# A hybrid attention/SSD layer: another order of the seven products, h kept in DRAM, and attention's result added by transfers

## The chip, the cores and the metric

The kernel runs on one core of a Trainium2 chip. The metric is the device time of one execution in microseconds (us); of several runs the median is given. Five engines work side by side, each through its own list of instructions in order: PE (TensorE: matrix products from SBUF into the PSUM banks), DVE (VectorE), ACT (ScalarE), POOL (GpSimd) and SP (SyncE, which here only issues transfers). An engine that has come to an instruction whose input isn't there waits with it, and all that stands behind it on that engine waits too. Transfers between DRAM and SBUF are issued on SP's queue (`dma` in the code) or on POOL's (`store`).

## The reference

One layer of a streaming encoder for two groups of requests, 1024 tokens of a prompt and 8 x 16 tokens of samples, 1152 in all, at a width of 1024:

```python
h = rms_norm(x, norm_g) * (1 + scale) + shift            # scale, shift, gate from silu(c) @ w_ada + b_ada
q, k, v, z_att, z_ssd, xbc, dt_raw, gates = split(h @ w_in)
att_branch = (attention(q, k, v) * silu(z_att)) @ w_att_proj           # 1024 -> 1024
y = ssd_scan(silu(conv(xbc)), dt, a) + d_skip * xs                     # 16 pairs of heads, 4 groups
ssd_branch = (rms_norm(y * silu(z_ssd)) * ssd_norm_g) @ w_ssd_proj     # 2048 -> 1024
g_att, g_ssd = split(gates)
merged = sigmoid(g_att) * att_branch + sigmoid(g_ssd) * ssd_branch
out = x + gate * (merged @ w_out)
```

Keys, values, convolution rows and the SSD state are outputs too.

## The kernel before

All is kept with channels on the 128 partitions and the 1152 tokens along a row, so that a tile of eight is 128 x 1152 in fp32 (576 KB). For precision a matrix product is made of three in fp16: both operands are split into a high and a low half (hi and lo; ScalarE rounds, L694 for weights and L2173 for operands; VectorE takes the remainder, L695 and L2175), and TensorE does hi x hi, hi x lo and lo x hi (L854, L855, L856).

**Stages.** First come h and its norm, then eight attention units (until about 650 us), then sixteen pairs of SSD heads (until about 1270), whose results go to DRAM (`att_d`, `y_d`). The last stage consists of dense products alone: eight plain blocks of gates (`gate_dense`), then **quads**. A quad, `quad_dense` (L834), computes two blocks of 128 output channels for all tokens from 1024 channels with seven products instead of eight: the operand pair is cut in four quarters (`quarters`), `differences` (L2182) forms their sums on VectorE, and the seven combinations of them are multiplied with seven combinations of weights (`quad_sums` prepares these early, in the SSD stage, and keeps them in DRAM as `sum_d`). One product has 4 steps of k, 2 banks of 288 columns and 3 matmuls each: 24 matmuls. There are twenty quads, five groups of four: the other gates, attention's projection (`att_dense`), the SSD projection in two halves of the operands (`ssd_dense(0)`, `ssd_dense(1)`), and the output projection (`out_dense`).

**Banks.** A quad uses three pairs of PSUM banks: `fore` (tag `d` or the double bank `s`, alternating from quad to quad), `side` (tag `g`) and `lone` (the one of `d` and `s` that `fore` is not). Products 0, 5, 6, 3 add up in `fore`, 4 and 2 in `side`, and 1 stands alone. Between them a bank is read out while its sum goes on: `kept` (L864) copies it to SBUF on ScalarE (L873) or adds it to a base on VectorE (L869, only in `ssd_dense(1)`), `joined` (L876) adds it to what was kept (L879). The next product on a bank can't start before it was read. The order was 0, 4, 5, 1, 6, 2, 3. The first quad of a group (`wide`) does products 0, 4 and 1 step by step of k side by side, since its operands come into being one after the other; it then runs 2 ahead of 6 and gives 3 a bank of its own.

**Operands.** `pieces` (L2194) turns a pair of tiles into the seven operands of one step of k: four sums of squares on ScalarE (L686, for a check of the range), three splits of 1152 columns and one of 576, and four additions on VectorE (L2184 to L2187). For the gates `h_pieces` (L2214) first puts h together, hi + lo, with one VectorE addition per tile (L2220, eight in all). For attention `att_prep` loads `att_d`; for the SSD `ssd_prep` loads `y_d` and scales it by the norm (L2261). The operands of the output stage come from `ssd_dense(1)`: in `second` the SSD result, held in tile a (which was loaded from `acc_d`, what the first half left), is multiplied by its gate (L2329), added to attention's result in tile m (L2330; m is loaded from `att_o`), and m goes to `pieces`. So the last step of k of the output stage waits for the last output of the last SSD quad.

**Weights.** SP loads raw weights into three places (`w_ahead`), four parts of 512 KB for a quad (two from `in_quad`, two from `sum_d`). `quad_split` splits a part into hi and lo; all seven buffers of a quad are taken at once, and given back at its end (`w_done`); `w_next` splits parts of the next quad at four points of a quad.

**Order.** The program is written by generators that run against a rough clock (`pause`), and then put in order: the class `Order` (L140) has a cost for each instruction and simulates the five engines. Whenever an engine is free, it takes of the instructions that are ready by the simulation, and ready by a safe margin if there are such, the one that stands earliest in the program (`at`); instructions in `fill` count as 600 places later. The resulting order of every engine is fixed. So the order follows planned times; on the chip an engine keeps it, even when a transfer comes later than planned. If a check of the values' range fails at the end, a general kernel would run; it doesn't here.

## Time and profile before

| | us |
|---|---|
| median of 3 runs (1721.12 to 1727.28) | 1721.31 |
| profiled execution | 1722.93 |
| its span, first to last instruction | 1721.0 |
| PE busy | 1677.3 |
| DVE busy | 1378.6 |
| ACT busy | 1061.5 |
| POOL busy | 391.5 |

The profile is of one execution. Busy times count a matmul from its start to its modelled end, and these overlap. A row of a group shows the line, the engine, the operation, the tiles (output <- input; `arena` is the whole of SBUF, `d`, `g` and `s` the PSUM banks), the shape, the count, the busy time and the mean of one, and after the bar the engine's idle time just before them and what ended it. A row of the timeline has the start, the length and in brackets the idle time before it.

### The profile page before, as it was taken

Reading aid. Unit: us, or ns where it says so; the run is one execution under the profiler, and the core shown is the slowest. Engines: PE = TensorE matmul, PEld = TensorE weight load, DVE = VectorE, ACT = ScalarE, POOL = GpSimd, SP = SyncE. Lnnn points to the kernel's source line nnn. Section 1 sums busy time; section 2 is a strip of 40 time slices with the busy share of each in tenths; the row PEclk is TensorE's granted clock in tenths of the full one; section 3 lists DMA queues with packets and bytes.
Section 4 is the critical chain, followed back from the end, with each engine's and each line's share of the span. In section 5 each row is a group of like instructions: output and inputs, shape, how many; then the busy total and the mean of one; then the engine's idle time right before and its main releaser. Section 6 shows DMA issues by size and latency. Waiting matters only on the chain.

```text
span 1721.0 us, 36673 instructions
## 1 busy us (share of the span) xinstructions
PE 1677.3 (97%) x14265; PEld 1122.4 (65%) x14265; DVE 1378.6 (80%) x2546; ACT 1061.5 (62%) x2130; POOL 391.5 (23%) x640
## 2 busy tenths in 40 slices
PE   7999999999999999999999999999999999999998
PEld 3556565556565556666666666666667677777776
DVE  6458767878777888989988989996898487878963
ACT  8766556566565567456655756666388575775550
POOL 0134233135133101322321333242231011110000
PEclk9999999999999999999999999999999999999999
DMA  9248789797988688686858767878658786777651
GB/s 383 83 120 212 169 227 228 169 230 189 210 227 189 168 190 228 184 220 199 196 182 271 231 184 242 238 217 272 226 166 294 266 292 207 254 284 259 221 194 58
DMA packets 299105, 369.16 MB, mean 214 GB/s; under 512 B 211676, under 2 KB 213096, under 8 KB 298920
## 3 DMA queue, kind: packets, MB, share of 16 engines
q1 hardware_dynamic: 281896, 307.65, 63.7%
q0 software_dynamic: 17024, 59.06, 9.4%
q8 instruction: 114, 1.87, 0.5%
q14 instruction: 71, 0.58, 0.1%
HBM read 244.08 MB, written 74.06 MB: 185 GB/s over the span
## 4 chain that ended last, share of the span: by engine, by line
PE 51%; DVE 18%; DMA 11%; ACT 11%; issue 7%; POOL 1%; SPq 1%; DVEq 0%; ACTq 0%; POOLq 0%
PE d L945 6%; PE d L948 6%; PE d L946 6%; PE d L998 5%; PE d L1000 5%; PE d L999 5%; ACT arena L686 3%; PE g L1604 2%; DVE arena L2175 2%; DMA arena<-in_quad_dram 2%; DMA arena<-acs_d 2%; DVE arena L695 2%; DVE arena L1802 2%; ACT arena L1988 1%; DMA arena<-sum_d 1%
## 5 line engine op out<-in xcount | busy, mean ns | idle before, releaser
L945 PE MATMUL d<-arena 128*128 128x384 f16 x1320 | 431.0, 327 | 1.4 <-ACT arena L1779 1.4
L948 PE MATMUL d<-arena 128*128 128x384 f16 x1320 | 430.3, 326 | 0.6 <-DVE arena L695 0.6
L946 PE MATMUL d<-arena 128*128 128x384 f16 x1320 | 430.3, 326 | 0.0
L686 ACT ACTIVATE arena<-arena 128x1024 bf16<-128x1024 f32 (+4 forms) x217 | 199.3, 918 | 141.9 <-DMA arena<-in_wall_dram 96.4
L695 DVE SCALAR_TENSOR_TENSOR arena<-arena 128x1024 f16<-128x1024 f32 (+2 forms) x157 | 181.7, 1165 | 42.4 <-ACT arena L694 42.2
L694 ACT ACTIVATE arena<-arena 128x1024 f16<-128x1024 f32 (+2 forms) x157 | 155.1, 994 | 66.5 <-DMA arena<-sum_d 33.1
L945 PEld LDWEIGHTS <-arena 128*128 128x128 f16 x1320 | 129.2, 98 | 90.2 <-issue 13.3
L998 PE MATMUL d<-arena 128*128 128x384 f16 (+1 forms) x568 | 186.8, 329 | 0.0
L1000 PE MATMUL d<-arena 128*128 128x384 f16 (+1 forms) x568 | 186.1, 328 | 0.0
L999 PE MATMUL d<-arena 128*128 128x384 f16 (+1 forms) x568 | 186.1, 328 | 0.0
L948 PEld LDWEIGHTS <-arena 128*128 128x128 f16 x1320 | 129.1, 98 | 86.3 <-DVE arena L695 1.0
L946 PEld LDWEIGHTS <-arena 128*128 128x128 f16 x1320 | 129.2, 98 | 78.5 <-issue 1.6
L1544 ACT ACTIVATE arena<-arena 128x640 f32<-128x640 f32 (+4 forms) x144 | 100.8, 701 | 63.5 <-DVE arena L1547 63.1
L855 PEld LDWEIGHTS <-arena 128*128 128x128 f16 x1120 | 109.7, 98 | 43.9 <-issue 16.3
L854 PE MATMUL d<-arena 128*128 128x288 f16 x440 | 126.3, 287 | 3.7 <-ACT arena L873 3.2
L856 PEld LDWEIGHTS <-arena 128*128 128x128 f16 x1120 | 109.8, 98 | 30.5 <-issue 2.7
L854 PEld LDWEIGHTS <-arena 128*128 128x128 f16 x1120 | 110.0, 98 | 29.5 <-issue 1.7
L855 PE MATMUL d<-arena 128*128 128x288 f16 x440 | 126.2, 287 | 1.1 <-DVE arena L2175 1.1
L856 PE MATMUL d<-arena 128*128 128x288 f16 x440 | 126.1, 287 | 0.0
L854 PE MATMUL s<-arena 128*128 128x288 f16 x360 | 102.9, 286 | 6.5 <-ACT arena L873 3.9
L1802 DVE SCALAR_TENSOR_TENSOR arena<-arena 128x1176 f32<-128x1176 f32 x72 | 103.2, 1434 | 5.5 <-ACT arena L1799 3.8
L2175 DVE SCALAR_TENSOR_TENSOR arena<-arena 128x1152 f16<-128x1152 f32 (+1 forms) x72 | 87.4, 1219 | 21.9 <-ACT arena L2173 21.7
(278 smaller groups left out, 3565.0 us busy)
## 6 DMA issues: line engine op xcount, KB each, us to landing
arena<-in_quad_dram SPq DMA_DIRECT2D x80, 512.0 KB, 5.7
arena<-in_wall_dram SPq DMA_DIRECT2D x77, 512.0 KB, 5.2
sum_d<-arena POOLq DMA_DIRECT2D x40, 512.0 KB, 4.7
arena<-sum_d SPq DMA_DIRECT2D x40, 512.0 KB, 4.8
arena<-acs_d SPq DMA_DIRECT2D x32, 576.0 KB, 5.8
arena<-in_kc_dram SPq DMA_DIRECT2D x64, 256.0 KB, 4.6
arena<-in_vc_dram SPq DMA_DIRECT2D x64, 256.0 KB, 2.9
arena<-in_wada_dram SPq DMA_DIRECT2D x24, 512.0 KB, 10.2
```

The source lines that it names most:

```text
L686: keep(nc.scalar.activation(junk[:, :n], x, AF.Square, scale=scale * n ** -0.5, accum_out=sums[:, c:c + 1]))
L694: keep(nc.scalar.activation(hi, x, AF.Copy, scale=scale))
L695: keep(nc.vector.scalar_tensor_tensor(lo, x, scale, hi, ALU.mult, ALU.subtract))
L854: nc.tensor.matmul(ps, wh, xh[:, c], start=first and k == 0, stop=False, skip_group_check=not first)
L855: nc.tensor.matmul(ps, wh, xl[:, c], start=False, stop=False, skip_group_check=not first)
L856: nc.tensor.matmul(ps, wl, xh[:, c], start=False, stop=k == 3, skip_group_check=not first)
L945: nc.tensor.matmul(ps, hi.r[:, wc], kh.r[:, tok], start=k == 0, stop=False)
L946: nc.tensor.matmul(ps, hi.r[:, wc], kl.r[:, tok], start=False, stop=False)
L948: nc.tensor.matmul(ps, lo.r[:, wc], kh.r[:, tok], start=False, stop=k == nk - 1)
L998: nc.tensor.matmul(ps, kh.r[:, tok], wh, start=k == 0, stop=False)
L999: nc.tensor.matmul(ps, kh.r[:, tok], wl, start=False, stop=False)
L1000: nc.tensor.matmul(ps, kl.r[:, tok], wh, start=False, stop=k == KT - 1)
```

## The change

- **Order of products** in a quad: 0, 4, (product 3 of the quad before), 5, 1, 2, 6, and product 3 is put off (`pending`, `flush`) to the next quad, where it runs behind 0 and 4 (in an interleaved first quad behind the first step of k). Ahead of the output stage, behind its last quad, and where the next operands aren't there yet, it runs at once. `lone` is now one bank `d` and one bank `g`. In an interleaved first quad the order of the rest is as in the others, with no bank of its own for product 3.
- **Priority**: instructions that read out banks (`quick`) count as 300 places earlier in the order, with a margin of 200 ns behind them.
- **Weights**: a quad's buffers are taken part by part and given back as soon as their last product is written (`w_used`); `w_next` may split for the quad after the next.
- **h**: `h_whole` makes the eight additions in pairs 1 to 4 of the SSD stage (as `fill`), stores the tiles to `h_d` on POOL's queue, and `h_pieces` loads them on SP's. The two places of `L_SUM` grow to 1152 columns for that, and the `pad` of 576 in `L_SSD` goes, by which the SSD's tiles no longer lie on the places of the last stage's.
- **Attention's result**: for three of the four quads of `ssd_dense(1)`, attention's result is no longer loaded into a tile and added on VectorE; a transfer on POOL's queue reads `att_o` and adds it to tile a (`accum_op`), and a goes to `pieces`, 9000 ns of the rough clock later. For the fourth quad the two tiles are loaded (`att_last`) and added as before.
- **Times**: the modulation's gate (`mod_gate`, eight loads of 512 KB) begins with the gates instead of with attention's projection; the pause ahead of the SSD norm's token sums is 12000 instead of 4500; loads ahead are released tile by tile.

```diff
@@ Order
+    FAST = 300
+    SAFE_FAST = 200.0
-            u["at"] = u["i"] + self.FILL * (u["ins"][0].name in self.fill)
+            u["fast"] = u["ins"][0].name in self.fast
+            u["at"] = u["i"] + self.FILL * (u["ins"][0].name in self.fill) - self.FAST * u["fast"]
-                    m = self.SAFE_DMA if v["dma"] else self.SAFE[u["eng"]]
+                    m = self.SAFE_DMA if v["dma"] else self.SAFE_FAST if u["fast"] else self.SAFE[u["eng"]]
@@ h
+    def h_whole(k):
+
+        b = yield from walloc(L_SUM, "s", NT)
+        fill.add(nc.vector.tensor_tensor(b.ap, hhi[k].ap, hlo[k].ap, ALU.add).ins.name)
+        yield from pause(1500)
+        store(h_d[k], b.ap)
+        stored(b)
...
-                nc.vector.tensor_tensor(t.ap, hhi[k].ap, hlo[k].ap, ALU.add)
+                dma(t.ap, h_d[k])
@@ quad_dense
+        if not ops:
+            yield from flush()
+        fore, side = bank(2 if odd else 0), bank(1)
...
         yield from product(0, fore)
         p1 = yield from kept(fore, 0, 0)
         yield from product(4, side)
         p5 = yield from kept(side, 1, 1)
+        yield from flush()
+        w_next(i)
         yield from product(5, fore, first=False)
+        w_used(i, 3, 4)
         u2 = yield from kept(fore, 0, 1)
         w_next(i)
-        if not wide:
-            lone = bank(0 if odd else 2)
+        lone = lone or bank(3)
         yield from product(1, lone)
+        w_used(i, 0, 1)
         yield from joined(0, 0, p1, lone)
         w_next(i)
-        if wide:
-            yield from product(2, side, first=False)
+        yield from product(2, side, first=False)
+        yield from joined(0, 1, u2, side)
         yield from product(6, fore, first=False)
+        w_used(i, 5, 6)
+        yield from joined(1, 1, p5, fore)
         w_next(i)
...
+        def rest():
             yield from product(3, fore, first=False)
+            w_used(i, 2)
             yield from evict(1, 0, [(g * HC, HC, ps) for g, ps in enumerate(fore)], None) or ()
-        w_done(i)
+        pending.append(rest)
@@ ssd_dense, second
-                m = yield from taken("att", c + o)
+                m = a if c < 6 else (yield from taken("att", o))
...
-                nc.vector.tensor_tensor(m.ap[:, tok], m.ap[:, tok], a.ap[:, tok], ALU.add)
+                if c < 6:
+                    nc.gpsimd.dma_start(a.ap[:, tok], att_o[c + o][:, tok], accum_op=ALU.add)
+                else:
+                    nc.vector.tensor_tensor(m.ap[:, tok], m.ap[:, tok], a.ap[:, tok], ALU.add)
...
-                        urgent.append(pieces(tiles["att"][c], m, out_ops, 0.5 * SM / (SA * SW)))
+                        def last(c=c, m=m):
+                            if c < 6:
+                                yield from pause(9000)
+                            yield from pieces(tiles["acc"][c] if c < 6 else tiles["att"][0], m, out_ops, 0.5 * SM / (SA * SW))
+                        urgent.append(last())
@@ the list of stages
+        if 1 <= p < 5:
+            items[-1][1].extend(h_whole(k) for k in range(2 * p - 2, 2 * p))
-    items.append((gates_dense(), [h_pieces(), att_prep()], [], 0.5))
-    items.append((att_dense(), [tile_loads(4, ("ga", gate_d, 0)), ssd_prep(), mod_gate()], [], 0.5))
+    items.append((gates_dense(), [mod_gate(), h_pieces(), att_prep()], [], 0.5))
+    items.append((att_dense(), [tile_loads(4, ("ga", gate_d, 0)), ssd_prep()], [], 0.5))
     items.append((ssd_dense(0), [], [], 0.5))
-    items.append((ssd_dense(1), [tile_loads(3, ("acc", acc_d, 0), ("gs", gate_d, 8), ("att", att_o, 0))], [], 0.5))
+    items.append((ssd_dense(1), [tile_loads(3, ("acc", acc_d, 0), ("gs", gate_d, 8)), att_last()], [], 0.5))
```

142 lines of the change are left out of this document (79 added, 63 removed).

## The prediction

> **What bounds the kernel now.** I read the page first, then busy time by stage, then what TensorE waited for, and only then single stalls with the engine that was late.
>
> ```profile
> span 1721.0 us, 36673 instructions
> PE 1677.3 (97%) x14265; PEld 1122.4 (65%) x14265; DVE 1378.6 (80%) x2546; ACT 1061.5 (62%) x2130; POOL 391.5 (23%) x640
> PEclk9999999999999999999999999999999999999999
> ...
> GB/s 383 83 120 212 169 227 228 169 230 189 210 227 189 168 190 228 184 220 199 196 182 271 231 184 242 238 217 272 226 166 294 266 292 207 254 284 259 221 194 58
> ```
>
> TensorE is busy for 1677.3 of 1721.0 us at nearly full clock. The change neither adds nor removes a matmul, so it can only win part of the missing 43.7 us. The stages, by the windows view (length, then busy us and count of PE, PEld, DVE, ACT, POOL; PEclk, DMA share, GB/s):
>
> ```profile
> 650.00:900.00 250.00, 249.40 (x1947) 165.65 (x1940) 226.07 (x335) 158.78 (x285) 67.80 (x101) 1.00 0.71 200
> 950.00:1000.00 50.00, 50.00 (x428) 33.52 (x427) 49.44 (x82) 37.70 (x71) 19.78 (x25) 1.00 0.79 217
> 1225.00:1275.00 50.00, 47.68 (x359) 30.14 (x357) 47.27 (x69) 32.31 (x59) 9.51 (x17) 1.00 0.48 165
> 1275.00:1358.00 83.00, 80.10 (x653) 63.61 (x651) 62.53 (x80) 70.49 (x134) 17.51 (x25) 1.00 0.70 233
> 1358.00:1444.00 86.00, 83.61 (x686) 64.60 (x684) 63.23 (x92) 48.72 (x93) 8.11 (x15) 1.00 0.77 280
> 1444.00:1530.00 86.00, 82.24 (x666) 64.87 (x665) 76.34 (x95) 64.26 (x123) 8.65 (x16) 1.00 0.74 248
> 1530.00:1620.00 90.00, 87.73 (x715) 69.68 (x713) 80.34 (x126) 50.56 (x79) 2.16 (x4) 1.00 0.72 250
> 1620.00:1650.00 30.00, 25.31 (x191) 19.09 (x190) 26.53 (x37) 18.68 (x33) 0.00 (x0) 0.94 0.71 246
> 1650.00:1713.00 63.00, 63.00 (x516) 50.22 (x514) 30.72 (x70) 15.78 (x32) 0.00 (x0) 1.00 0.35 122
> ```
>
> The rows from 1275 to 1713 are the twenty quads (gates, attention, SSD twice, output). Their idle time is length less PE busy: 2.90 + 2.39 + 3.76 + 2.27 + 4.69 + 0 = 16.0 us. The last row also gives the price of a matmul where nothing is missing: 63.00 / 516 = 0.122 us, so a product of 24 matmuls lasts 2.93 us and a quad of seven 20.5 us. In the quads TensorE waited for (us in total, times, longest):
>
> ```profile
> PE s L854 <- ACT arena L873: 3.9, 3, 2.3
> PE d L854 <- ACT arena L873: 3.2, 3, 1.7
> PE g L854 <- ACT arena L873: 2.4, 1, 2.4
> PE s L854 <- DVE arena L879: 1.3, 1, 1.3
> PE g L854 <- DVE arena L869: 1.2, 1, 1.2
> PE g L855 <- DVE arena L2175: 1.2, 1, 1.2
> PE d L855 <- DVE arena L2175: 1.1, 1, 1.1
> ```
>
> These are waits for a PSUM bank being read out: by the copy L873, or by the adds L869 and L879. The two on L2175 are different: the last operand of the output stage isn't split yet. Why the copies were late stands on ScalarE (start, length; idle before, releaser):
>
> ```profile
> 1347.62 0.68 ACT L2173 ACTIVATE arena<-arena 128x576 f16<-128x576 f32 x1 [3.73 <-DMA gate_d<-arena]
> 1350.71 1.16 ACT L2173 ACTIVATE arena<-arena 128x1152 f16<-128x1152 f32 x1 [1.81 <-DVE arena L2185]
> 1351.78 0.69 ACT L873 ACTIVATE arena<-d 128x288 f32<-128x288 f32 x2
> 1372.72 1.16 ACT L2173 ACTIVATE arena<-arena 128x1152 f16<-128x1152 f32 x1 [8.51 <-DVE arena L2261]
> 1373.79 0.69 ACT L873 ACTIVATE arena<-g 128x288 f32<-128x288 f32 x2
> 1632.00 1.06 ACT L694 ACTIVATE arena<-arena 128x1024 f16<-128x1024 f32 x1 [2.38 <-DMA arena<-in_quad_dram]
> 1633.78 0.69 ACT L873 ACTIVATE arena<-s 128x288 f32<-128x288 f32 x2
> ```
>
> The copies cost only 0.69 us a pair; they stood behind an operand split (L2173) or a weight split (L694) that itself waited, up to 8.51 us, for a transfer or another engine. TensorE lost less, because it had products that needed no such bank.
>
> **The change part by part.** *Order of products.* Product 3 of a quad moves behind products 0 and 4 of the next, and product 2 ahead of 6, so outside the four-step interleaved first quads one more product, 2.93 us, lies between a bank's use and its reuse. The longest wait on a bank, 2.4 us, is shorter. The interleaved first quads gain no such cover; they have only the new priority (evictions sorted 300 places ahead, and the plan's margin behind them 200 ns, not 300). Their waits, in the timeline of PE:
>
> ```profile
> 1286.78 0.28 PE L854 MATMUL s<-arena 128*128 128x288 f16 x1 [1.20 <-ACT arena L873]
> 1374.23 0.28 PE L854 MATMUL g<-arena 128*128 128x288 f16 x1 [2.35 <-ACT arena L873]
> 1460.58 0.28 PE L854 MATMUL s<-arena 128*128 128x288 f16 x1 [0.47 <-ACT arena L873]
> 1554.79 0.28 PE L854 MATMUL s<-arena 128*128 128x288 f16 x1 [0.65 <-DVE arena L869]
> ```
>
> They sum to 4.7 us. With the 4.7 us of 1620 to 1650 set aside, 16.0 - 4.7 - 4.7 = 6.6 us lie in the other quads. The bounds there are 0 (the waits grow with the cover) and 6.6; since every one is shorter than the added cover, I take 6.3. Of the first quads' 4.7 I take half, 2.3, between 0 and all: priority helps a copy behind a long queue, not one behind an instruction that the engine has already begun to wait with. Each vanished gap also saves the 0.16 us by which a matmul's row (0.28) outlasts its interval (0.122), since the busy column counts that as work: some ten gaps, 1.6 us.
>
> *h.* Eight adds leave the end of the SSD stage, where VectorE is busy 47.27 of 50 us and TensorE idle for 2.3, and go to pairs 1 to 4.
>
> ```profile
> L2220 DVE TENSOR_TENSOR arena<-arena 128x1152 f32<-128x1152 f16 x8 | 10.8, 1351 | 0.1
> L2330 DVE TENSOR_TENSOR arena<-arena 128x576 f32<-128x576 f32 x16 | 11.9, 750 | 0.0
> arena<-att_o SPq DMA_DIRECT2D x8, 576.0 KB, 8.0
> att_o<-arena POOLq DMA_DIRECT2D x16, 288.0 KB, 4.6
> arena<-sum_d SPq DMA_DIRECT2D x40, 512.0 KB, 4.8
> ```
>
> 10.8 us of VectorE go away there; I take half of the 2.3 us back, 1.2 (bounds 0 and 2.3). In 650 to 900 VectorE has 250 - 226 = 24 us free, and 950 to 1000 shows TensorE full beside a VectorE at 49.44 of 50, so the adds there cost 0 to 2 us, taken 0.5; without that cover they would cost their 10.8. Eight stores on POOL's queue and eight loads of 576 KB on SP's are new; 4.7 MB in the 50 us at a DMA share of 0.48 make some 94 GB/s more, which fits. If a load of a pair is late, the SP queue holds the weight loads behind it and the first gates quad waits: 0 when hidden, up to 8.0 us by the slowest load row; hidden, since each pair is asked for before the eight plain gate blocks end. The modulation's eight weight loads (512 KB each) move to the same stretch, out of the attention stage; with both, the added rate is about 180 GB/s on 165, 345 in all, below the 383 of the page's first slice, so nothing is charged.
>
> *Attention's result.* Twelve of the sixteen adds L2330 (0.75 us each, 9 us of VectorE) become accumulating transfers on POOL's queue, and six of the eight loads of att_o on SP go. No row shows an accumulating transfer. The nearest are 4.6 us (a plain store of the same 288 KB) and 8.0 (a load of twice the bytes); below 4.6 nothing speaks for a gain. I take 6. For channels 4 and 5, the last that use it, the operand starts later by two products, 5.9 us, plus 6, less the 0.75 of the add: 11 us (10 to 13). What slack is there is read on VectorE at the boundary:
>
> ```profile
> 1616.93 0.75 DVE L2187 SCALAR_TENSOR_TENSOR arena<-arena 128x576 f32<-128x576 f32 x1
> 1628.67 0.81 DVE L2325 TENSOR_TENSOR arena<-arena,d 128x288 f32<-128x288 f32 x2
> 1637.03 1.36 DVE L2175 SCALAR_TENSOR_TENSOR arena<-arena 128x1152 f16<-128x1152 f32 x1 [2.11 <-ACT arena L2173]
> ```
>
> The third operand was nearly ready at 1616.93 and the last one starts at 1628.67: 11 to 12 us of slack, just used up. So the boundary keeps its 4.7 us and I charge 0.5 more (bounds: 2.4 less, the wait for in_quad at 1632.00, to 2 more). By the Trainium skill, page "DMA: Bandwidth & Descriptors", section "Anatomy of one DMA — SWDGE (gpsimd) path", a POOL transfer lasts 2.0 us plus its bytes at 436 GB/s, an estimate of 2.7 us for 288 KB; the row's 4.6 us for a store is longer. By it the sum would be 0.5 us lower.
>
> *Weights.* Buffers are taken part by part and given back after the product that used them, and a quad two ahead may be split; ScalarE's 2.38 us for in_quad at 1632.00 is what this aims at. It is inside the 2.4 above; nothing more is taken. The longer pauses of the norm's sums cost nothing: their results are wanted a stage later.
>
> *End.* In the very last quad product 3 follows 6 on the same bank with nothing between but the add L879 (two of the 0.81 us pair's kind): 0.4 to 0.8 us new, 0.5 taken.
>
> **Sum.** -6.3 - 2.3 - 1.6 - 1.2 + 0.5 + 0.5 + 0.5 = -9.9 us. The profiled execution lasted 1722.93 us, 1.9 more than its span, and becomes 1713.0; it is 1.6 above the median of the runs, 1721.31, which becomes 1711.4. No change can be told within 0.5%, 8.6 us, so the forecast lies just past that line.
>
> **The rivals.**
>
> *The waits only move* (0.26). The blocked ScalarE is in-order, and the transfers stay as slow: if L873 queues behind another L694 or L2173, only half of 6.3 + 2.3 + 1.6 comes, 5.1 us, and 1.2 - 1.5 leaves it at that: 4.8 less, 1716.5. For it speaks the 8.51 us idle at 1372.72, longer than any cover; against it that TensorE lost but 2.35 there.
>
> *The boundary goes too* (0.11). Earlier splits and 9 us less VectorE work also fill 1620 to 1650. That adds 4.7 us and the half clock:
>
> ```profile
> 1640.00:1650.00 10.00, 9.50 (x66) 7.05 (x66) 8.95 (x13) 7.92 (x15) 0.00 (x0) 0.83 0.81 257
> ```
>
> 0.17 of 10 us at half rate is a stretch of 3.4 us, which costs 1.7. With 2.3 more from the first quads it comes to 1711.4 - 8.7 = 1702.7. Against it speaks that the last operand hangs on the very last product, as before. The Trainium skill, "TensorE: Matmul & The Clock Gate", section "HAM oscillation — how this bites in real kernels", asks for no idle gap over some 3.4 us; here the clock fell after gaps of at most 2.3 us, so the measured row decides.
>
> *Slower: accumulating transfers that don't keep up* (0.13). Four fall into each quad of 20.5 us, one per 5.1 us. If the queue works them one after another, it falls behind from 5.1 us each on; at 6.5 us the twelfth is 12 x 6.5 - 61.5 = 16 us late, and the output stage's third operand with it. TensorE starves for about 16 us plus two stretches at half clock, 3.4: 1711.4 + 19.4 = 1730.8. For it: 4.6 and 8.0 stand on either side of 5.1. Against: plain transfers of this kernel overlap, with 4.8 us to land and a DMA share of 0.7 to 0.8.
>
> **How the numbers follow.** Forecast 0.50 (its own range 1707 to 1716), waits move 0.26, boundary 0.11, slower 0.13. The line at 1712.7 cuts the forecast at about 0.35 to 0.15. Faster: 0.35 + 0.11 + 0.01 of the waits = 0.47; same: 0.15 + 0.25 + 0.01 = 0.41; slower 0.12. The range, 1702 to 1726, holds the forecast, the moved waits, most of the faster case and the accumulating transfers up to half their price.
>
> **What would show it.** Right: idle PE in 1275 to 1620 falls from 11.3 to under 4 us, waits on L873 nearly vanish except in interleaved quads, the eight adds of h show between 650 and 900 with PE still full. Wrong: accumulates that land after more than 8 us, ScalarE idle behind sum_d or in_quad with PE waiting on L873 behind it, more than 5 us idle where the output stage starts, or idle PE around 1225 to 1290 behind loads of h_d.

## The result, and the profile after

The change made the kernel slower: 1747.51 us median (1741.92 to 1755.48, 4 runs) against 1722.24 us of the kernel before beside it, a ratio of 1.0135 with a 95% interval of 1.0105 to 1.0164. Forecast were 1711.4 us and a range up to 1726; both miss. The profiled execution of after lasted 1745.13 us, its span is 1743.3 us, 22.3 more than before.

The head of the page of after, with the same rows as were shown of before:

```profile
span 1743.3 us, 36714 instructions
...
PE 1682.6 (97%) x14265; PEld 1124.0 (64%) x14265; DVE 1369.4 (79%) x2527; ACT 1058.6 (61%) x2123; POOL 395.2 (23%) x660
```

The page hardly shows a change: VectorE has 9 us less to do, as meant, and TensorE the same 14265 matmuls. One has to go by stages. The windows view of after, cut at its own stages (columns: stretch, length, busy us and count of PE, PEld, DVE, ACT, POOL; PEclk, DMA share, GB/s):

```profile
650.00:900.00 250.00, 249.71 (x1951) 165.85 (x1952) 232.26 (x338) 160.53 (x287) 65.54 (x104) 1.00 0.73 210
900.00:1225.00 325.00, 308.62 (x2384) 203.65 (x2383) 279.47 (x429) 191.22 (x361) 94.05 (x138) 0.99 0.78 233
1225.00:1275.00 50.00, 50.00 (x433) 34.79 (x432) 40.55 (x77) 22.00 (x42) 10.39 (x18) 1.00 0.79 281
1291.00:1388.00 97.00, 91.15 (x723) 69.64 (x722) 61.06 (x88) 74.16 (x136) 15.69 (x27) 0.96 0.73 240
1388.00:1471.00 83.00, 82.47 (x672) 65.51 (x671) 64.54 (x86) 49.58 (x91) 8.01 (x16) 1.00 0.72 247
1471.00:1557.00 86.00, 82.86 (x672) 65.52 (x671) 77.39 (x95) 67.97 (x127) 8.90 (x17) 1.00 0.78 269
1557.00:1600.00 43.00, 42.96 (x351) 34.28 (x351) 27.84 (x45) 15.70 (x25) 6.22 (x8) 1.00 0.87 280
1600.00:1652.00 52.00, 41.40 (x327) 31.98 (x326) 41.42 (x66) 28.53 (x48) 5.08 (x6) 0.95 0.79 222
1652.00:1736.00 84.00, 83.82 (x676) 66.19 (x674) 51.62 (x99) 29.25 (x53) 0.00 (x0) 0.99 0.38 124
```

And the same windows of before for the stretch that the prediction had not looked at:

```profile
900.00:1225.00 325.00, 323.25 (x2551) 216.42 (x2550) 288.36 (x451) 195.14 (x368) 102.41 (x140) 1.00 0.80 240
```

Three stretches lost time. From 900 to 1225, still in the SSD stage, TensorE is busy 14.6 us less than before. The gates (1291 to 1388) have 5.85 us without a matmul and a clock of 0.96. The end of the SSD projection (1600 to 1652) has 10.6 us without one. Attention's projection (0.53 idle) and the output (0.18 idle) are close to full.

To compare kernels I use marks: the start of the first quad's first matmul, and then of every 672nd matmul of 288 columns (four quads of 168), counted in the trace. The SSD projection's second half and the output are taken together, since the wait between them falls on either side of the mark. The marks of all kernels, in us, with the ratio to the kernel before beside them:

```
kernel                  ratio  [95%]              first  gates +    ssd   ssd(1) +  tail
                                                  quad   attention  (0)   output
before                                            1275.5   176.0    87.0   174.3     8.2
after                   1.0135 [1.0105, 1.0164]   1291.1   180.1    86.2   178.3     7.6
h_back                  1.0073 [1.0044, 1.0102]   1287.6   170.2    88.6   181.4     9.4
pause_back              1.0049 [1.0018, 1.0081]   1285.1   174.5    85.2   180.8     8.5
modgate_back            1.0093 [1.0065, 1.0122]   1295.0   173.1    86.1   178.6     7.7
acc_back                1.0086 [1.0053, 1.0119]   1294.2   183.7    86.6   171.5     7.7
acc_back_late           1.0052 [1.0025, 1.0079]   1293.2   181.8    88.1   169.4     7.3
row_on_pool             1.0126 [1.0093, 1.0159]   1295.7   180.7    86.9   181.4     8.3
order_alone             0.9918 [0.9892, 0.9944]   1280.1   173.8    84.7   171.6     6.5
order_late_pieces       0.9970 [0.9949, 0.9991]   1279.9   176.2    84.8   172.8     6.9
order_acc               1.0029 [1.0010, 1.0048]   1275.5   173.7    85.1   180.8     9.9
order_modgate           0.9999 [0.9966, 1.0032]   1290.5   166.1    90.6   171.8     6.5
pause_alone             1.0003 [0.9972, 1.0034]   1281.1   178.5    86.8   173.3     8.3
h_alone                 1.0082 [1.0050, 1.0115]   1285.5   183.4    89.1   173.5    12.6
h_early_only            1.0087 [1.0058, 1.0115]   1287.7   176.2    89.7   173.2    12.2
places_alone            1.0015 [0.9985, 1.0046]   1279.8   175.5    87.4   174.4     8.4
early_adds_old_places   1.0097 [1.0067, 1.0127]   1288.3   175.5    89.0   174.0     9.6
early_adds_no_store     1.0063 [1.0035, 1.0091]   1286.9   177.0    87.4   173.6     8.4
early_adds_on_pool      1.0132 [1.0097, 1.0167]   1297.1   179.1    88.4   174.5    10.1
order_h_on_pool         1.0058 [1.0022, 1.0094]   1299.3   175.8    87.3   168.3     6.6
```

After's row less before's: +15.6 before the first quad, +4.1, -0.8, +4.0, -0.6: the 22.3 us. In order_modgate and h_back the modulation's matmuls run, wholly or mostly, ahead of the first quad and count in the first column; their place in attention is worth 8.2 us (90.9 us for that group in order_alone, 82.7 in order_modgate). A mark comes from a single trace, and may differ from another's by some us without a cause in the edit: the kernels from before without h's additions or the modulation's move start their quads between 1275.5 and 1281.1.

### The profile page after: what moved, and what is told of

Its sections match the earlier page's. It is cut to its first block, busy times and chain, and to the rows that moved or that the text cites. A ratio compares the mean times of both kernels' runs of the same rounds, so it can differ in the third digit from the quotient of the medians.

```text
span 1743.3 us, 36714 instructions
## 1 busy us (share of the span) xinstructions
PE 1682.6 (97%) x14265; PEld 1124.0 (64%) x14265; DVE 1369.4 (79%) x2527; ACT 1058.6 (61%) x2123; POOL 395.2 (23%) x660
## 5 line engine op out<-in xcount | busy, mean ns | idle before, releaser
L690 ACT ACTIVATE arena<-arena 128x1024 bf16<-128x1024 f32 (+4 forms) x217 | 199.0, 917 | 128.2 <-DMA arena<-in_wall_dram 76.8
L885 PE MATMUL d<-arena 128*128 128x288 f16 x400 | 115.1, 288 | 10.5 <-DVE arena L910 9.9
L885 PE MATMUL g<-arena 128*128 128x288 f16 x400 | 115.1, 288 | 6.9 <-ACT arena L2406 5.3
L2022 ACT ACTIVATE arena<-arena 128x128 f32<-128x128 f32 x288 | 89.8, 390 | 43.9 <-DMA arena<-acs_d 40.4
L886 PE MATMUL d<-arena 128*128 128x288 f16 x400 | 115.2, 288 | 0.0
L887 PE MATMUL g<-arena 128*128 128x288 f16 x400 | 115.2, 288 | 0.0
L886 PE MATMUL g<-arena 128*128 128x288 f16 x400 | 115.2, 288 | 0.0
```

Of the source, the lines that this page charges most:

```text
L690: keep(nc.scalar.activation(junk[:, :n], x, AF.Square, scale=scale * n ** -0.5, accum_out=sums[:, c:c + 1]))
L885: nc.tensor.matmul(ps, wh, xh[:, c], start=first and k == 0, stop=False, skip_group_check=not first)
L886: nc.tensor.matmul(ps, wh, xl[:, c], start=False, stop=False, skip_group_check=not first)
L887: nc.tensor.matmul(ps, wl, xh[:, c], start=False, stop=k == 3, skip_group_check=not first)
```

## The experiments

### Each part undone in after, and all four

Five kernels: h's part undone (additions at the gates again, old places, the spare columns back); the pause back to 4500; the modulation's gate back in attention's stage; attention's result loaded and added on VectorE again; and all four undone together, which leaves the order of products, the priority and the weights' buffers (`order_alone`).

```diff
# h_back (the places and the spare columns also go back)
...
-        if 1 <= p < 5:
-            items[-1][1].extend(h_whole(k) for k in range(2 * p - 2, 2 * p))
...
-                dma(t.ap, h_d[k])
+                nc.vector.tensor_tensor(t.ap, hhi[k].ap, hlo[k].ap, ALU.add)
# pause_back
-                yield from pause(12000)
+                yield from pause(4500)
# modgate_back
-        yield from ready(lambda: ssd_all[NPAIR])
+        yield from ready(lambda: len(att_ops) >= 1)
...
-    items.append((gates_dense(), [mod_gate(), h_pieces(), att_prep()], [], 0.5))
+    items.append((gates_dense(), [h_pieces(), att_prep()], [], 0.5))
...
# acc_back (the loads of attention's result come back too)
...
-                if c < 6:
-                    nc.gpsimd.dma_start(a.ap[:, tok], att_o[c + o][:, tok], accum_op=ALU.add)
-                else:
-                    nc.vector.tensor_tensor(m.ap[:, tok], m.ap[:, tok], a.ap[:, tok], ALU.add)
+                nc.vector.tensor_tensor(m.ap[:, tok], m.ap[:, tok], a.ap[:, tok], ALU.add)
...
```

> The changed kernel, but h is put together on VectorE at the gates as before (no early additions, no stores and loads of h_d, the pad and the places of 1024 columns are back). If the additions and their stores, or the shifted tiles, cost the 15.6 us that the SSD stage lost (first quad matmul at 1291.1 instead of 1275.5), the first quad starts within 3 us of 1275.5 and the time is about 1730. If the norm's longer pause (rows stored late on SP's queue) did it, the first quad still starts later than 1286 and the time stays above 1740. If any new order of the long stage costs some us by chance, it lies in between, with stalls at other places.

> The changed kernel with the pause ahead of the SSD norm's sums at 4500 again instead of 12000. If SP's queue, held for 10.6 us by the norm's row, is the cause, the 11 us wait of ScalarE for acs_d near 1014 to 1025 goes, the first quad starts 8 to 15 us earlier and the time is about 1735. If h's additions and stores are the cause, the first quad stays at 1286 or later and the time at 1740 to 1755.

> The changed kernel with the modulation's gate back in the attention stage. The gates' group of quads took 96.8 us instead of 85.5 and attention's 83.3 instead of 90.5. If moving it cost the wait of 5.3 us on its copy and the half clock behind that, the two groups together fall from 180.1 to 173 to 176 and the time by 4 to 7 us. If the wait only changes its place, as before at 1374 (2.35 us), together they stay at 178 to 181 and the time is unchanged.

> The changed kernel with attention's result loaded and added on VectorE as before, no accumulating transfer. If the late pieces behind these transfers cost the second SSD group its time (94.4 us instead of 85.1), it falls to 84 to 87 us and the time by 7 to 10 us, while the output group may grow back from 83.9 towards 86. If VectorE's load is what counts there, the group stays at 92 or more, since 9 us of additions come back.

> The changed kernel with all four undone together: h, the norm's pause, the modulation's gate and attention's result as before. What is left is the order of products, the priority of evictions and the weights' buffers. If these do what the prediction said (some 8 to 10 us less waiting in the quads) and the four parts carry the whole loss, the time is 8 to 12 us below the kernel before, the first quad starts at 1272 to 1278 and the twenty quads take 427 to 431 us instead of 437.3. If the order itself costs something, or a new order of the list loses by chance wherever it is made, the time is equal to the kernel before or above it.

Measured: each part undone alone wins something, by the medians of the ratios 0.62% (h), 0.86% (pause), 0.42% (modulation) and 0.49% (accumulating transfers). They add up to 2.4%; all four undone win 2.17%. So no single edit made the kernel slow. Each of these differences carries the intervals of two kernels, some 0.4% together, so the modulation's and the transfers' stand at the edge of what can be told. The gains of these two fall where they were expected: gates and attention take 173.1 instead of 180.1 us, the SSD projection's second half 83.6 instead of 94.4. With the pause undone the time is the expected one, but the quads start 6.0 us earlier, not 8 to 15. With h undone the time of 1739.1 us lies between the two cases that were set out, 1730 and above 1740. The part that remains, `order_alone`, beats both kernels: 0.9918 of before, 14 us by the interval's middle, 10 to 19 by its ends. Its profiled execution is but 4.3 us shorter (span 1716.7): its quads start 4.6 us later, take 7.2 less, and the tail is 1.7 shorter. The profiled execution of before was one of the short ones (1722.93 us; beside order_alone before's median was 1729.53), so the traces hold less of the gain than the runs, and the rest isn't located. Its windows at the five groups of quads:

```profile
1280.00:1363.00 83.00, 82.60 (x675) 65.80 (x674) 62.76 (x81) 73.32 (x135) 16.97 (x26) 1.00 0.72 241
1363.00:1454.00 91.00, 88.18 (x724) 68.15 (x722) 66.65 (x99) 48.57 (x89) 8.20 (x16) 1.00 0.78 272
1454.00:1538.00 84.00, 81.96 (x669) 65.21 (x667) 72.73 (x89) 65.06 (x123) 8.52 (x16) 1.00 0.76 267
1538.00:1622.00 84.00, 82.78 (x676) 65.97 (x675) 76.97 (x123) 44.10 (x73) 1.08 (x2) 1.00 0.74 256
1622.00:1710.00 88.00, 84.71 (x678) 66.56 (x676) 54.87 (x102) 31.87 (x58) 0.00 (x0) 0.98 0.44 148
```

Idle are 0.4 + 2.8 + 2.0 + 1.2 + 3.3 = 9.8 us, where before had 16.0, and the quads take 430.1 us against 437.3. The copies' waits fall from 9.5 us to 3.6, by PE's waits on L904 (the old L873) in this list of order_alone's waits from 1275 to 1712. The four that are left stand in interleaved first quads (at 1289, 1379, 1465 and 1633).

```profile
PE s L885 <- ACT arena L904: 3.6, 4, 1.4
PE g L1111 <- DVE arena L910: 1.9, 1, 1.9
PE s L886 <- DVE arena L2209: 1.8, 1, 1.8
```

### Attention's result: the transfer, or the later operand

Where the transfer is used, the operand's split comes later in the program (9000 ns of the rough clock). Two kernels take the lateness alone, one of after and one of order_alone; a third adds the transfers to order_alone.

```diff
# acc_back_late (on acc_back) and order_late_pieces (on order_alone)
-                        urgent.append(pieces(tiles["att"][c], m, out_ops, 0.5 * SM / (SA * SW)))
+                        def last(c=c, m=m):
+                            if c < 6:
+                                yield from pause(9000)
+                            yield from pieces(tiles["att"][c], m, out_ops, 0.5 * SM / (SA * SW))
+                        urgent.append(last())
# order_acc (on order_alone, with the later split as above and the loads for the fourth quad as in after)
...
+                if c < 6:
+                    nc.gpsimd.dma_start(a.ap[:, tok], att_o[c + o][:, tok], accum_op=ALU.add)
```

> The changed kernel without accumulating transfers (loads and additions as before), but with the pause of 9000 ahead of the pieces kept. If the lateness of the pieces in the program, not the transfer, costs the second SSD group its 9 us, it stays at 92 to 96 us. If the transfer's landing does, the group takes 83 to 86 us, as with the additions alone put back (83.6).

> The order of products, priority and weights' buffers alone (as in the run that had all four undone), and the pieces of the output stage put 9000 ns later in the program, without accumulating transfers. The second SSD group and the output took 83.7 and 87.9 us without the pause, 84.5 and 84.9 with it in the changed kernel. If this adds to the order's gain, the ratio to the kernel before is 0.989 to 0.991; if the gain there was chance, it is 0.992 or more.

> The same order alone, with the accumulating transfers and their pause as in the changed kernel. If the wait of ScalarE on the accumulated tile is what cost the second SSD group, that group takes 92 to 96 us instead of 83.7, the output group 84 to 86 instead of 87.9, and the ratio to the kernel before rises from 0.992 to 0.995 to 0.998. If the transfers only cost in company with the other three parts, the group stays below 87.

Measured: in the two groups concerned the lateness is hardly seen (169.4 against 171.5 us in acc_back; 172.8 against 171.6 in order_alone). By the runs acc_back_late is 0.34% faster than acc_back, but order_late_pieces is 0.52% slower than order_alone, and the intervals of these two don't overlap. Of the 3.9 us between their traces 2.4 stand in gates and attention. So the lateness, or the other order that is planned with it, isn't shown to be free. The transfers come on top: order_acc takes 8.0 us more than order_late_pieces in the two groups (180.8 against 172.8) and 0.59% more by the runs, some 10 us; against order_alone it is 9.2 us and 1.11%. Taking them out of after wins 6.8 to 8.9 us (171.5 and 169.4 against 178.3). The chain is seen in the timelines of order_acc. On ScalarE (start, length; in brackets idle before and releaser):

```profile
1623.46 0.68 ACT L690 ACTIVATE arena<-arena 128x576 bf16<-128x576 f32 x1 [3.96 <-DMA arena<-att_o]
```

On VectorE:

```profile
1626.93 1.36 DVE L2209 SCALAR_TENSOR_TENSOR arena<-arena 128x1152 f16<-128x1152 f32 x1 [4.07 <-ACT arena L2207]
```

On TensorE, just behind it:

```profile
1628.70 0.40 PE L885 MATMUL d<-arena 128*128 128x288 f16 x1 [6.48 <-DVE arena L910]
```

ScalarE comes to the range check L690 of an operand and stands 4 us, since the transfer hasn't landed: it is the twelfth, issued at 1615.73 and landed at 1623.35. Its split L2207 follows late, VectorE stands with the remainder L2209, and behind L2209 in VectorE's order is the addition L910 that reads out the bank. TensorE waits 6.48 us for a bank, not for the operand. In after the same happens at 1604, on VectorE and TensorE:

```profile
1602.41 1.36 DVE L2209 SCALAR_TENSOR_TENSOR arena<-arena 128x1152 f16<-128x1152 f32 x1 [4.92 <-ACT arena L2207]
1603.68 0.81 DVE L910 TENSOR_TENSOR arena<-arena,d 128x288 f32<-128x288 f32 x2
```

```profile
1604.18 0.28 PE L885 MATMUL d<-arena 128*128 128x288 f16 x1 [2.47 <-DVE arena L910]
...
1651.10 0.40 PE L885 MATMUL d<-arena 128*128 128x288 f16 x1 [5.90 <-DVE arena L910]
```

The wait of 5.90 us at 1651.10 has the same L2207, L2209 and L910 behind it. On ScalarE the view names the last quad's own addition as what was waited for:

```profile
1645.85 0.68 ACT L690 ACTIVATE arena<-arena 128x576 bf16<-128x576 f32 x1 [3.53 <-DVE arena L2375]
```

But the same instruction also waits for the twelfth transfer, issued at 1638.71, and that landed at 1645.75, only 0.1 us before the addition ended. So the transfer alone would have held ScalarE nearly as long; which of the two set the time, this trace can't tell. The transfers took about the time that the prediction took for them. Groups and issues of after:

```profile
L2373 POOL DMA_DIRECT2D arena<-att_o x12 | 10.2, 852 | 67.4 <-DVE arena L2371 50.0 <-PE g L887 9.9 <-issue 7.5
```

```profile
att_o<-arena POOLq DMA_DIRECT2D x16, 288.0 KB, 3.9
arena<-att_o POOLq DMA_DIRECT2D x12, 288.0 KB, 6.7
```

They land after a median of 6.7 us, the single ones after 4.3 to 8.9, and the last ones no later than the first.

### h: the whole of it, the early part, and what in it

In the kernel before, h's part was put in alone; then its early half alone (additions and stores in pairs 1 to 4, new places; the gates still add for themselves, so nothing reads what is stored).

```diff
# h_alone (on before, with h_whole as in after; h_early_only is the same without the last two lines)
-    L_SSD = arena.set_layout(Z0, [("X", 1, XW), ("R", 2, 1184), ("t", 8, 36), ("pad", 1, 576), ("T", 9, NT), ("Y", 1, 1184), ("H", 1, 1024),
+    L_SSD = arena.set_layout(Z0, [("X", 1, XW), ("R", 2, 1184), ("t", 8, 36), ("T", 9, NT), ("Y", 1, 1184), ("H", 1, 1024),
-    L_SUM = arena.set_layout(E0 - NSUM * 1024, [("s", NSUM, 1024)])
+    L_SUM = arena.set_layout(E0 - NSUM * NT, [("s", NSUM, NT)])
+        if 1 <= p < 5:
+            items[-1][1].extend(h_whole(k) for k in range(2 * p - 2, 2 * p))
...
-                nc.vector.tensor_tensor(t.ap, hhi[k].ap, hlo[k].ap, ALU.add)
+                dma(t.ap, h_d[k])
```

> The kernel before with h's part alone (early additions, stores, loads, places of 1152 columns, no pad). If h's part alone disturbs the SSD stage, the first quad starts 8 to 16 us later than 1275.5 and the time is 8 to 16 us longer. If it needs the longer pause of the norm beside it, the first quad starts within 4 us of 1275.5 and the time is the same within 4 us.

> The kernel before with h's additions and stores in pairs 1 to 4 and the shifted places, but the gates still add hi and lo themselves and load nothing. If the early additions, stores and places cost the 14 us that h's part alone cost, the time stays 10 to 16 us above the kernel before. If the loads of h_d at the gates and what they order differently behind them on SP's queue do (SP stood 14 us with the norm's row at 1285, TensorE then 6.4 us at 1311), it is within 5 us of the kernel before.

Measured: 1.0082 and 1.0087. The early half alone has the whole price. In its trace, 18.1 us longer than before's, 12.2 us come before the first quad (1287.7 against 1275.5); 4.0 more stand behind the last matmul and 2.7 in the SSD projection's first half, and for these no run gives a reason. With the loads of h beside it gates and attention take 183.4 us in h_alone, 176.2 without them, and one wait stands out in h_alone's timeline of TensorE:

```profile
1311.11 0.40 PE L863 MATMUL s<-arena 128*128 128x288 f16 x1 [6.37 <-ACT arena L882]
```

It isn't the loads alone: modgate_back has the same loads, and the modulation in attention as h_alone has it, and its two groups take 173.1 us.

The first suspect for the early part was SP's queue, which in after is held for 10.6 us by the row of the norm (`row_on_pool` issues it from POOL's queue, in after):

```diff
-        dma(d1.rearrange("a b -> (a b)").rearrange("(p j) -> p j", p=P), v[1])
+        store(d1.rearrange("a b -> (a b)").rearrange("(p j) -> p j", p=P), v[1])
```

> The changed kernel, with the one row of each SSD norm (1152 numbers) stored from POOL's queue instead of SP's, so that SP cannot stand and wait for POOL's small operations there; nothing else differs. If SP held for 10.6 us by that row is what delayed acs_d and the weights, the stall of 3.8 us near 1030 goes, the SSD stage ends 6 to 12 us earlier than 1291 and the time falls to 1733 to 1740. If h's part disturbs the stage by its additions and places alone, the SSD stage ends at 1288 or later and the time stays at 1742 or more.

Measured: 1.0126, first quad at 1295.7, no better than after. SP's queue in after has this wait, which ends before 1020:

```profile
SPq L1415 <- POOL arena L660: 10.6, 1, 10.6
```

In row_on_pool it is gone, but SP stands around 1020 for the landing of the same row,

```profile
SPq L1807 <- DMA yb<-arena: 7.9, 1, 7.9
```

and behind it ScalarE's longest wait for `acs_d` is 10.3 us, against 11.1 in after, and TensorE's stall of 3.8 us is the same. So taking the row's issue off SP doesn't help. Nor does a wait of this length have to cost anything: SP in before stands as long between 1020 and 1040, where TensorE is full.

```profile
SPq L1976 <- DVE arena L2089: 11.2, 1, 11.2
```

Next the early half was taken apart, in the kernel before.

```diff
# places_alone: the spare columns go, nothing else
-    ("t", 8, 36), ("pad", 1, 576), ("T", 9, NT)
+    ("t", 8, 36), ("T", 9, NT)
# early_adds_old_places: additions and stores, all places as before, 1024 of each 1152 columns
...
+        b = yield from walloc(L_SUM, "s", 1024)
+        fill.add(nc.vector.tensor_tensor(b.ap, hhi[k].ap[:, :1024], hlo[k].ap[:, :1024], ALU.add).ins.name)
# early_adds_no_store (on h_early_only)
-        yield from pause(1500)
-        store(h_d[k], b.ap)
# early_adds_on_pool (on h_early_only); order_h_on_pool: the same with the whole of h's part, on order_alone
-        fill.add(nc.vector.tensor_tensor(b.ap, hhi[k].ap, hlo[k].ap, ALU.add).ins.name)
+        fill.add(nc.gpsimd.tensor_tensor(b.ap, hhi[k].ap, hlo[k].ap, ALU.add).ins.name)
```

> The kernel before with one edit: the 576 spare columns between the SSD stage's small tiles and its T tiles are gone, so nine of the T tiles, Y, H and g lie 576 columns lower in the arena. No instruction is added or taken away. 'It is the place of the tiles': the SSD stage gets the longer time of the run with h's early part (first quad matmul at 1285 to 1288 us, against 1275.5 in before), ratio 1.006 to 1.009. 'It is the eight additions': first quad matmul at 1274 to 1278, ratio 0.998 to 1.002.

> The kernel before with h's eight early additions and their stores, but with every place where it was: the spare columns stay and the two places for the quads' sums keep 1024 columns, so only 1024 of each 1152 columns are added and stored (the gates still add h themselves, nothing reads the stored copy). 'It is the eight additions with their stores in those two places': first quad matmul at 1284 to 1288, ratio 1.006 to 1.009. 'It is the place of the tiles': first quad matmul at 1275 to 1278, ratio 0.999 to 1.002.

> The run with h's early part alone (ratio 1.0087), without the eight stores, whose 576 KB each are not written: the additions on VectorE, the longer places and the shifted tiles stay. 'It is the stores' (POOL's queue and the moving of 4.5 MB in the SSD stage): first quad matmul back at 1275 to 1279, ratio 0.999 to 1.002. 'It is the additions or the places': 1284 to 1288, ratio 1.006 to 1.009.

> The run with h's early part alone (ratio 1.0087, first quad matmul at 1287.7 us), with one word changed: the eight early additions run on GpSimd instead of VectorE. The places, the shifted tiles, the stores and the waits for the places stay. 'It is VectorE's time' (its idle time from 640 us to the first quad stayed at 68 to 71 us in before and in all three runs with the additions, while its busy time grew by 13 to 15 us): first quad matmul at 1276 to 1281, ratio 0.999 to 1.004. 'It is the places, the slots of the plan or the moved fills': 1284 to 1289, ratio 1.006 to 1.009. If GpSimd's additions of 1152 columns take several us each, or slow VectorE's own, the time can also grow beyond that.

> The order, priority and weights' part (ratio 0.9918 alone, first quad matmul at 1280.1 us) with the whole of h's part, the early additions on GpSimd: stored, and loaded for the gates, so that VectorE is rid of 10.8 us of additions before the gates. 'It is VectorE's time': first quad matmul at 1270 to 1277, as these 10.8 us lie ahead of it; ratio 0.986 to 0.992, less what h's loads cost the gates (93 us with them in the run of h alone, against 83). 'It is the places or the moved fills': first quad at 1284 to 1290, ratio 0.996 to 1.002.

Measured: the places alone cost nothing that can be told (1.0015, first quad at 1279.8, inside the spread of the other kernels). The additions with every place where it was cost everything (1.0097, 1288.3). Without the stores most of it stays (1.0063, 1286.9). So it is the additions, 10.7 us of VectorE, or what comes with them: another planned order of the stage, and their turns in the two places of `L_SUM`, which they share with the weights' sums in all of these runs. The windows from 640 us to the first quad, of before

```profile
640.00:1275.50 635.50, 630.83 (x4970) 418.95 (x4967) 565.06 (x860) 393.64 (x728) 179.71 (x258) 1.00 0.74 218
```

of h_early_only

```profile
640.00:1287.70 647.70, 636.39 (x4994) 421.50 (x4993) 580.12 (x873) 399.10 (x736) 183.83 (x272) 1.00 0.74 223
```

and of early_adds_old_places

```profile
640.00:1288.30 648.30, 636.01 (x4976) 421.64 (x4975) 578.33 (x871) 395.38 (x732) 180.24 (x271) 0.99 0.74 222
```

show VectorE idle for 635.5 - 565.06 = 70.4, 67.6 and 70.0 us. It has 70 us free in this stage, but the additions did not go into them: the stage grew by 12.2 and 12.8 us, about as much as VectorE's work (15.1 and 13.3), and TensorE's idle time grew from 4.7 to 11.3 and 12.3 us.

If VectorE's time alone is the cause, additions on another engine should cost little. They cost more there: 1.0132, first quad at 1297.1, and 1299.3 in order_h_on_pool. This group of early_adds_on_pool shows what each took:

```profile
L701 POOL TENSOR_TENSOR arena<-arena 128x1152 f32<-128x1152 f16 x8 | 21.8, 2724 | 20.3 <-PE s L1715 10.6 <-DMA h_d<-arena 7.0 <-DMA sum_d<-arena 1.8
```

2.7 us each, twice VectorE's 1.35, with 20.3 us of standing before them. The expected times failed, but the run doesn't clear VectorE, for its own work got longer, as one of the expectations had allowed. Its window has 577.64 us of VectorE for 862 instructions, against 565.06 for 860 in before:

```profile
640.00:1297.10 657.10, 639.36 (x4973) 421.98 (x4971) 577.64 (x862) 395.52 (x732) 193.03 (x278) 0.99 0.73 218
```

The timelines of the two engines show where: beside an addition on GpSimd an instruction of VectorE took 3.18 us, and the next of the same line 1.43.

```profile
781.65 2.36 POOL L701 TENSOR_TENSOR arena<-arena 128x1152 f32<-128x1152 f16 x1
782.08 3.18 DVE L1811 SCALAR_TENSOR_TENSOR arena<-arena 128x1176 f32<-128x1176 f32 x1
785.84 1.43 DVE L1811 SCALAR_TENSOR_TENSOR arena<-arena 128x1176 f32<-128x1176 f32 x1
```

So the additions cost VectorE some 10 us or more on either engine. Shown is that they lengthen the stage on either engine, that the tiles' places cost nothing that can be told, and the stores little. VectorE's time fits all of these runs. Not shown is by which instruction the delay runs on, and the planned order and the turns in `L_SUM` aren't ruled out.

### The modulation's gate and the pause, each alone

```diff
# order_modgate (on order_alone)
-        yield from ready(lambda: len(att_ops) >= 1)
+        yield from ready(lambda: ssd_all[NPAIR])
...
-    items.append((gates_dense(), [h_pieces(), att_prep()], [], 0.5))
-    items.append((att_dense(), [tile_loads(4, ("ga", gate_d, 0)), ssd_prep(), mod_gate()], [], 0.5))
+    items.append((gates_dense(), [mod_gate(), h_pieces(), att_prep()], [], 0.5))
+    items.append((att_dense(), [tile_loads(4, ("ga", gate_d, 0)), ssd_prep()], [], 0.5))
# pause_alone (on before)
-                yield from pause(4500)
+                yield from pause(12000)
```

> The order, priority and weights' part (ratio 0.9918 alone; gates 82.9 us and attention 90.9 us by the quads' marks) with one edit more: the modulation's gate moved from attention to the gates, as in after. If its move costs what undoing it in after gave back (7 us over the two groups), gates and attention take 178 to 181 us together and the ratio is 0.995 to 0.998. If it cost in after only because h's loads and the longer pauses stood beside it, the two take 173 to 175 us and the ratio is 0.991 to 0.993.

> The kernel before with the norm's pause at 12000 alone. If the pause alone puts the norm's row in front of the next loads on SP's queue, SP waits there for POOL for 10 us at two of the groups, ScalarE waits for acs_d behind it, and the time is 8 to 15 us longer. If it only does so together with h's part, the time is the same within 4 us.

Measured: the modulation's move costs order_alone all its gain, 0.9999 against 0.9918; by the marks of the two traces 8.7 us to the end of the SSD projection's first half (1547.3 against 1538.5). Neither expectation named where: only 2.8 of them have come by the end of attention (1456.7 against 1453.9), the other 5.9 fall into that half, where TensorE has 6.7 us without a matmul (2.0 in order_alone) and ScalarE stands 13.5 us for weights of `sum_d` by this list of order_modgate's waits,

```profile
ACT arena L698 <- DMA arena<-sum_d: 13.5, 5, 6.1
```

against 3.6 in order_alone's:

```profile
ACT arena L698 <- DMA arena<-sum_d: 3.6, 3, 1.9
```

Why these weights are late there isn't shown. In after the move stood in the open in the gates. ScalarE's timeline:

```profile
1301.19 0.69 ACT L690 ACTIVATE arena<-arena 128x576 bf16<-128x576 f32 x1 [2.22 <-DMA arena<-att_d]
...
1302.68 0.58 ACT L2406 ACTIVATE arena<-g 128x512 f32<-128x512 f32 x1
```

TensorE's:

```profile
1303.31 0.40 PE L885 MATMUL g<-arena 128*128 128x288 f16 x1 [5.28 <-ACT arena L2406]
```

The modulation's sums lie in a pair `g` that the quads need as `side`; its copy L2406 stood on ScalarE behind operands that waited for attention's loads, and TensorE waited 5.28 us. The same copy holds TensorE for 6.1 us in acc_back and in acc_back_late; in modgate_back the gates have no such wait. Then came a stretch at a lower clock:

```profile
1300.00:1310.00 10.00, 6.69 (x32) 4.28 (x32) 5.28 (x5) 6.62 (x13) 6.59 (x10) 0.66 0.82 290
```

The pause alone does nothing (1.0003), though taking it out of after wins 0.86%. It costs only in the company of the other edits; which one, no run tells.

## Why the prediction was wrong, by its steps

- **Order, priority and weights, -6.3 - 2.3 - 1.6 us: right in its mechanism.** In order_alone the waits on copies are gone but for interleaved first quads, as said. The size is less sure: 6.2 us less idle time in the quads and 7.2 us less for them in the traces, 14 us (10 to 19) by the runs. Idle time up to the output stage falls from 11.3 to 6.5 us, not under 4 as named; 1.9 of it is a new wait of the modulation's matmuls (L1111). After shows the gain too, where nothing covers it: attention's group is nearly full. The rival that the waits only move (5.1 us of gain) lies below the runs' interval; by the traces alone it couldn't be told from the forecast.
- **h, "the adds there cost 0 to 2 us, taken 0.5": the largest failure.** The check named for it came true: from 650 to 900 TensorE is busy 249.71 of 250 us, and the eight additions stand in this stretch, as the group of after from 640 to 900 shows:

```profile
L704 DVE TENSOR_TENSOR arena<-arena 128x1152 f32<-128x1152 f16 x8 | 10.7, 1351 | 6.1 <-DMA h_d<-arena 4.0 <-DMA sum_d<-arena 2.1
```

  The bill came in the next 325 us, 14.6 us of TensorE in after, and some 12 us ahead of the first quad with the early half alone (8 us against places_alone, whose quads start at 1279.8). The step took VectorE's 24 free us of 250 as cover. They were not: VectorE's idle time ahead of the quads stayed (70.4 and 67.6 us) and the work came on top. The prediction's own fallback, "without that cover they would cost their 10.8", is about what was measured. The row of 50.00 beside 49.44 of 50 showed that TensorE can stay full for a while beside a full VectorE, not that more work is free.
- **h's relief at the end of the stage, -1.2: not shown.** In the last 50 us ahead of the first quad TensorE is full in after, where before had 2.3 us idle. But it is full there in order_alone too, where the additions stand at the gates as before:

```profile
1241.00:1291.00 50.00, 50.00 (x376) 31.77 (x374) 44.17 (x67) 32.77 (x62) 8.97 (x16) 1.00 0.82 288
1230.00:1280.00 50.00, 50.00 (x375) 31.79 (x374) 48.44 (x69) 34.57 (x64) 10.04 (x18) 1.00 0.50 173
```

  The first row is after's, the second order_alone's. So the idle time of before there isn't shown to come from the additions. The loads of h, feared there, did no harm in that stretch.
- **"Nothing is charged" for the modulation's loads: failed.** It priced bytes per second, and these fitted (281 GB/s from 1225 to 1275). What cost in after was the work that hangs on the loads: a copy that came late in ScalarE's order, and the bank it held, 5.28 us of TensorE. In order_modgate the cost falls elsewhere, behind late weights, and why is open. Alone the move takes 0.8% from order_alone; taken out of after it gives back 0.42%.
- **Attention's result, "I charge 0.5 more": failed in the step from the landing to the end.** 6 us were taken for the landing, 6.7 were measured, and the transfers did not fall behind one another (one of twelve took more than the 8 us named as a sign, 8.9). The slack of 11 to 12 us was read on VectorE, from the third operand to the last: it asked when the operand's work is due, not what else stands behind it. But ScalarE came to that operand before it had landed and stood, VectorE stood behind ScalarE, and the bank additions L910 of the running quad were behind that: 9.2 us on order_alone in the traces, in place of 0.5, or 8.0 where the later split alone is set aside. The slower rival had the right place and sign, and about half of its 19.4 us, by another mechanism, so that is luck. The page of the Trainium skill named there, "DMA: Bandwidth & Descriptors", section "Anatomy of one DMA — SWDGE (gpsimd) path", gave an estimate of 2.7 us for 288 KB; the trace's 6.7 for an adding transfer disagrees, and so do the 3.9 and 5.3 of plain stores of the same bytes.
- **"The longer pauses cost nothing": right alone (1.0003), wrong in after (0.86%).** Why is open.
- **End, +0.5:** the tail behind the last mark is 7.6 us in after and 6.5 in order_alone, against 8.2 in before, so no loss is seen there.
- **The sum** added terms of parts that share ScalarE and VectorE as though each met the kernel of before. The order's gain was right to within the runs' interval. What made the forecast wrong are three costs taken as 0 to 0.5 us each, which measured some 12 (h), 8.7 (modulation) and 9.2 us (attention's result) in the traces.

## What to carry to other kernels

Idle time of an engine is not by itself a reserve. Here 10.7 us of additions beside 70 us of idle VectorE cost their full length, and putting them on GpSimd cost more; so cost added work at its full length until a run shows that it hides, and look for the bill in the stage after the one where it was put. When an operand comes later, ask not whether its reader has slack, but what stands behind the waiting instruction on each engine that it passes; here that was the addition that frees a PSUM bank. When a bundle of edits comes out slower, undo each one and then all: here the four that moved work and transfers hid a reorder that was worth 0.8%.

## What the runs showed of the hardware that was not expected

An adding transfer of 288 KB took a median of 6.7 us to land, against 3.9 and 5.3 us for the plain stores of the same bytes in the same run (`att_o`, `acc_d`). That isn't the price of adding as far as shown: plain stores that were issued just ahead of the transfers, by the view from 1540 to 1660, took as long.

```profile
arena<-att_o POOLq DMA_DIRECT2D x12, 288.0 KB, 6.7
acc_d<-arena POOLq DMA_DIRECT2D x5, 288.0 KB, 6.9
```

What differs is GpSimd's time for the issue, 0.85 us each against 0.54 (though the plain stores of `sum_d`, 512 KB, take 0.81):

```profile
L2352 POOL DMA_DIRECT2D acc_d<-arena x16 | 8.6, 539 | 76.1 <-DVE arena L910 42.2 <-ACT arena L2351 24.3 <-ACT arena L904 5.4
```

An addition on GpSimd lengthened VectorE's own work beside it: 3.18 us in place of 1.43 in the lines above.

TensorE's waits of 5.28 us in after and 6.48 us in order_acc cost more than their length. Behind order_acc's wait of 6.48 us the matmuls of 288 columns start every 0.24 us, not every 0.122:

```profile
1628.70 0.40 PE L885 MATMUL d<-arena 128*128 128x288 f16 x1 [6.48 <-DVE arena L910]
1628.90 0.45 PE L886 MATMUL d<-arena 128*128 128x288 f16 x1
1629.14 0.45 PE L887 MATMUL d<-arena 128*128 128x288 f16 x1
```

So it goes on until 1633.94, for 22 intervals, which makes some 2.6 us. The granted clock of the window around it is 0.87:

```profile
1600.00:1640.00 40.00, 30.49 (x224) 22.89 (x223) 32.04 (x48) 17.48 (x31) 1.70 (x2) 0.87 0.55 168
```

The rule on gaps named in the prediction (the Trainium skill, "TensorE: Matmul & The Clock Gate", section "HAM oscillation — how this bites in real kernels", some 3.4 us) agrees with this row, as it did not with the one of before. It doesn't agree with order_alone's last window either, whose clock is 0.98 although TensorE's longest wait in the quads is 1.9 us.
